# First operands of a merge split ahead of the last gate tile, in a longer-lived gate pool

## The chip, the cores and the metric

The kernel runs on one core of one Trainium2 chip. The metric is the device time of one execution in microseconds (us). Five engines work in parallel, each through its own list in order: PE (TensorE, matrix products), DVE (VectorE), ACT (ScalarE), POOL (GpSimd) and SP (SyncE, which here issues nearly all DMA transfers). They synchronise by semaphores.

## The reference

One inference step of a hybrid decoder layer (one layer here) for 1024 prompt tokens and 32 sampled tokens (8 sequences of 4), width 1024, float32:

```python
h = rmsnorm(x, norm_mix_w)
p = h @ w_in          # split into q, k, v | conv input u | z, a, b | gates g_a, g_b
o_a = stick_breaking(q, k, v)           # 8 heads of 64, causal
o_b = gated_delta(conv(u), z, a, b)     # 4 heads of 128
y_a = o_a.reshape(bsz, t_len, SB_DIM) @ w_pa.astype(F32)
y_b = o_b @ w_pb.astype(F32)
mix = (jax.nn.sigmoid(g_a) * y_a + jax.nn.sigmoid(g_b) * y_b) @ w_o.astype(F32)
x = x + mix
hm = rmsnorm(x, norm_mlp_w)
x = x + jnp.square(jax.nn.relu(hm @ w_up.astype(F32))) @ w_down.astype(F32)
```

In stick-breaking attention the weight of key j for query i is sigmoid(z_ij) times the product of (1 - sigmoid(z_ik)) over the keys k between j and i: a product scan in place of a softmax.

## The kernel before, in words

All 1056 tokens stand in the columns of transposed activations; the features are in the 128 partitions. The columns are cut into four chunks `CX` of 256, 256, 256 and 288. Every dense product keeps float32 accuracy by three products on PE: both operands are split into a high part (a copy by ACT, rounded to the matmul's type) and a low part (a subtraction by DVE, `x - hi`), and hi*hi, lo*hi and hi*lo are added in PSUM. So each operand needs an ACT copy and a DVE subtraction before its first use. For the weights `load_w` does this (tiles `ws`, `wh`, `wl`).

The stages that matter here:

- The gate projection. Sixteen tiles (8 feature tiles j, for gate A with b = 0 and gate B with b = 1), each of four chunks with 24 matmuls (`pd_g`). The input is `xh`, `xl` in the pool `xp`. Each result goes through a sigmoid into a tile `gt` and by DMA to DRAM (`gA_d`, `gB_d`). Tiles `gt` are in the pool `fk`, under the tag "ft" with four buffers, as are the transposed residual blocks `xs`, which are loaded (`xr`), transposed by DVE and stored (`xT_d`).
- The attention, 64 blocks (head h, query block i). A block is: score products `sc`, ACT's sigmoid into `s`, a mask and `1 - s` on POOL (`am`), the product scan `pr` and a product with `s` on DVE, PE's transposes into `wt` (evacuated by ACT), and the products with the values, `po`, which ACT copies into a staging tile `oT` of the head. After the fourth copy of a head two DMA stores take `oT` to `o_d`. `pipeline` runs the blocks with fills between them: five gate tiles and the residual blocks up to block 34 (`SPLIT`), after that the second merge.
- The second merge, w_pb (tiles `pb`). Its operand is the delta-net branch, `o_d[4:8]`, loaded per chunk as `ofb0` to `ofb3` and split into `obh`, `obl`. Result times gate B goes into `tb`. It is called second after its place in the formula; in time it comes before the other.
- The first merge, w_pa (tiles `pa`), whose operands are `oa0` to `oa2` (loaded as `ofa0` to `ofa2`, split into `oah`, `oal`) and `oa3`, which the last attention heads write directly. Then `w_o`, the norm and the MLP.

Nothing in the code orders the engines' lists by hand. The tile framework plans them: it simulates the program with its own times and puts each engine's instructions in the order in which they come up, with some raised by `tc.high_priority()`. A tile that reuses the memory of another waits for the last reader of that one, a DMA store included. Pools are stacked, so where a pool is opened decides its address, and when it is closed what may follow there.

Of the kernel before, what the change touches and what calls it, by code (L numbers as in the profile page):

```python
# [8 lines left out]
F32 = mybir.dt.float32  # L9
F32R = mybir.dt.float32r  # L10
I32 = mybir.dt.int32
I64 = mybir.dt.int64
AF = mybir.ActivationFunctionType
ALU = mybir.AluOpType
# [4 lines left out]
P = 128  # L19
# [3 lines left out]
T = NP + NS  # L23
# [3 lines left out]
CX = [(0, 256), (256, 256), (512, 256), (768, 288)]  # L27
# [5 lines left out]
NC = NP // P  # L33
# [5 lines left out]
def hybrid_step(ctx, tc, x_prompt, x_sample, cache_k, cache_v, page_table, state_conv, state_ssm,  # L39
# [7 lines left out]
    def pool(name, bufs=1, stack=ctx, side=None, space=None):  # L47
        kw = {} if space is None else {"space": space}
        if side is not None:
            kw["side"] = side  # L50
        return stack.enter_context(tc.tile_pool(name=name, bufs=bufs, reuse_waits="tile", **kw))

    cst = pool("cst")
    wctx = ExitStack()
    wpool = pool("wpool", 2, stack=wctx)
    kctx = ExitStack()
    keep = pool("keep", stack=kctx)
    dr = ctx.enter_context(tc.tile_pool(name="dr", bufs=1, space=DRAM))
# [33 lines left out]
    for t in range(9):  # L92
        xn = sp.tile([P, D], F32, tag="xn", name=f"xn{t}", bufs=7)
        n = P if t < 8 else NS
# [9 lines left out]
            w0s.append(st)  # L104
    ident = cst.tile([P, P], F32, name="ident")
    make_identity(nc, ident)
    ones = cst.tile([P, P], F32, name="ones")
    V.memset(ones, 1.0)
    powc = cst.tile([P, 2], F32, name="powc")
# [75 lines left out]
    xctx = ExitStack()  # L185
    zctx = ExitStack()
    zp = pool("zp", stack=zctx)
    xp = pool("xp", stack=xctx)
    xhc, xlc = [None] * 4, [None] * 4
    for c in (3, 2, 1, 0):  # L190
        xhc[c] = xp.tile([P, KT, CX[c][1]], F32R, name=f"xh{c}")
        xlc[c] = xp.tile([P, KT, CX[c][1]], F32R, name=f"xl{c}")
    fk = pool("fk", stack=xctx)
    w0 = []
    for t in range(9):
        n = P if t < 8 else NS
# [169 lines left out]
        return (1536 + i * P, f"u{name}", evac), cv  # L366

    def z_job(h):
        z = zp.tile([P, T + 48], F32, tag="zz", name=f"z{h}")[:, 0:T]

        def evac(c, o, n, pt):
            S_.activation(z[:, o:o + n], pt[:, :n], AF.Copy)
            if c == 3:
                S_.activation(z, z, AF.Silu)
                G.tensor_copy(zs[:, h, :], z[:, NP:T])
                SY.dma_start(z_d[h], z[:, 0:NP])

        return 3072 + h * P, f"z{h}", evac
# [424 lines left out]
    NFT = 4  # L803
# [189 lines left out]
    def values_of(blk):  # L993
        hh, i = blk
        p, a = hh // 2, hh % 2
        vn = vns[p]
        if hh < 6:
            if i % 2 == 0:
                return
            m = i // 2  # L1000
            if m == 0:
                oTs[hh] = ak.tile([P, NC // 2, P], F32, tag="oT", name=f"oT{hh}")
            rs = slice(64 * a, 64 * a + 64)
            po = gtile(f"po{hh}_{m}")
            for b in range(2 * m + 2):
                for r in range(2):
                    if b > 2 * m + r:
                        continue
                    PE.matmul(po[64 * r:64 * r + 64, 0:P], lhsT=vn[:, b, rs], rhs=wts[hh, 2 * m + r][:, b * P:(b + 1) * P],  # L1009
                              start=(b == 0), stop=(b == 2 * m + r))  # L1010
            S_.activation(oTs[hh][:, m, :], po[:, 0:P], AF.Copy)
            if m == NC // 2 - 1:
                for r in range(2):
                    SY.dma_start(o_d[p, rs, 0:NP].rearrange("d (m r c) -> d r m c", r=2, c=P)[:, r],
                                 oTs[hh][64 * r:64 * r + 64])
            return
        if a == 0:
            return
        po = gtile(f"po6_{i}")
        for b in range(i + 1):  # L1020
            for x in range(2):
                rs = slice(64 * x, 64 * x + 64)
                PE.matmul(po[rs, 0:P], lhsT=vn[:, b, rs], rhs=wts[6 + x, i][:, b * P:(b + 1) * P], start=(b == 0), stop=(b == i))
        cs_ = slice(i * P, (i + 1) * P)
        S_.activation(oah3[:, cs_], po[:, 0:P], AF.Copy)
        V.tensor_tensor(oal3[:, cs_], po[:, 0:P], oah3[:, cs_].bitcast(F32), op=ALU.subtract)
# [30 lines left out]
    def pipeline(x0, x1, fill):  # L1057

        done = 0
        for x in range(x0, x1):  # L1060
            stage_a(x + LAG)
            upto = len(fill) * (x + 1 - x0) // (x1 - x0)
            stage_b(x, fill[done:upto])
            done = upto
# [14 lines left out]
    def residual_step(t):  # L1079
        n = P if t < 8 else NS  # L1080
        xn = ak.tile([P, D], F32, tag="xr", name=f"xr{t}", bufs=1)
        SY.dma_start(xn[:n], x_prompt[0, t * P:(t + 1) * P, :] if t < 8 else x_sample.rearrange("s t d -> (s t) d"))

        xs = fk.tile([P, D], F32, tag="ft", name=f"xs{t}", bufs=NFT)
        V.transpose(xs[:n], xn[:n])
        for a in range(n // 32):
            o = t * P + 32 * a
            SY.dma_start(xT_d[:, :, o:o + 32].rearrange("k (b i) j -> i (k b) j", i=32),
                         xs[32 * a:32 * a + 32].rearrange("i (b j) -> i b j", j=32))
# [16 lines left out]
    for x, (j, b) in enumerate(gjobs[11:]):  # L1106
        for c in range(len(CX)):
            fills.append(lambda j=j, b=b, c=c: gate_step(j, b, c))
            t = 4 * x + c
            if t % 2 == 1 and t >= 3:  # L1110
                fills.append(lambda t=(t - 3) // 2: residual_step(t))
    pipeline(0, SPLIT, fills)
    ofb0 = zp.tile([P, 4, 256], F32, tag="zz", name="ofb0")
    SY.dma_start(ofb0, o_d[4:8, :, 0:256].rearrange("k p c -> p k c"))
    xctx.close()
    tbctx = ExitStack()
    oa3 = pool("oa3", stack=tbctx)
# [17 lines left out]
    tbs = [tbp.tile([P, T], F32, name=f"tb{j}") for j in range(KT)]  # L1135
    obctx = ExitStack()
    obp = pool("obp", stack=obctx)
    obh, obl = [None] * 4, [None] * 4

    def ob_tiles(c):  # L1140
        obh[c] = obp.tile([P, 4, CX[c][1]], F32R, name=f"obh{c}")
        obl[c] = obp.tile([P, 4, CX[c][1]], F32R, name=f"obl{c}")

    for c in range(len(CX)):
        ob_tiles(c)
    for c, (o, n) in enumerate(CX):
        if c == 0:
            st = ofb0
        else:
            if c == 1:  # L1150
                st = z2p.tile([P, 4, 288], F32, tag="zz", name="ofb1")[:, :, 0:256]
            elif c == 2:
                st = obp.tile([P, 4, 256], F32, name="ofb2")
            else:
                st = z2p.tile([P, 4, 288], F32, tag="zz", name="ofb3")
            mark = SY.dma_start(st, o_d[4:8, :, o:o + n].rearrange("k p c -> p k c"))
        with tc.high_priority():
            S_.activation(obh[c], st, AF.Copy)
            V.tensor_tensor(obl[c], st, obh[c].bitcast(F32), op=ALU.subtract)
        if c == 2:  # L1160
            for j in range(2):
                SY.dma_start(tbs[j], gB_d[j])
# [39 lines left out]
    gap = pool("gap", 2, stack=gaps, side="right")  # L1202
    oA = [None] * 3 + [(oah3, oal3)]
    for k in range(3):
        oh = oap.tile([P, T], F32R, name=f"oah{k}")
        ol = oap.tile([P, T], F32R, name=f"oal{k}")
        if k == 2:
            st = oap.tile([P, T], F32, name="ofa2")
            SY.dma_start(st, o_d[k])
        else:  # L1210
            st = ofa[k]
        S_.activation(oh, st, AF.Copy)
        V.tensor_tensor(ol, st, oh.bitcast(F32), op=ALU.subtract)
        oA[k] = (oh, ol)
# [25 lines left out]
    gaps.close()  # L1240
    oactx.close()
    tbctx.close()
    zctx.close()

    kctx.close()
# [481 lines left out]
```

## Time and profile before

| | before |
|---|---|
| runs | 1691.89, 1692.62, 1697.1 us (median 1692.62) |
| profiled execution | 1702.95 us |
| its span (first to last instruction) | 1701.2 us |
| granted TensorE clock, mean | 0.994 |
| busy: PE, DVE, ACT, POOL | 97%, 69%, 46%, 14% |

The profiled execution is a run of its own, 10.3 us over the median of the others. A start time is given in us from the start of the span. A row of the timeline names start, duration, engine, source line, operation, output<-inputs and shape; rows of the same kind next to each other are joined ("x4"). In brackets stand the idle time of the engine ahead of it and what ended it. SPq is the queue of SP, where a DMA transfer is issued; it takes longer to land.

### The profile page before, as it was taken

Reading aid. Unit: us, or ns where it says so; the run is one execution under the profiler, and the core shown is the slowest. Engines: PE = TensorE matmul, PEld = TensorE weight load, DVE = VectorE, ACT = ScalarE, POOL = GpSimd, SP = SyncE. Lnnn points to the kernel's source line nnn. Section 1 sums busy time; section 2 is a strip of 40 time slices with the busy share of each in tenths; the row PEclk is TensorE's granted clock in tenths of the full one; section 3 lists DMA queues with packets and bytes.
Section 4 is the critical chain, followed back from the end, with each engine's and each line's share of the span. In section 5 each row is a group of like instructions: output and inputs, shape, how many; then the busy total and the mean of one; then the engine's idle time right before and its main releaser. Section 6 shows DMA issues by size and latency. Waiting matters only on the chain.

```text
span 1701.2 us, 34901 instructions
## 1 busy us (share of the span) xinstructions
PE 1656.6 (97%) x14046; PEld 1603.9 (94%) x14046; DVE 1174.4 (69%) x2363; ACT 778.3 (46%) x1556; POOL 229.7 (14%) x249
## 2 busy tenths in 40 slices
PE   7999999999999999999999999999999999999998
PEld 6999999999998789988999999999999999999998
DVE  6666676877334327889776488887777688688964
ACT  5453434343424225555533356554445563444455
POOL 2120111110004226665300000000000000000000
PEclk9999999999999999999999999999999999999999
DMA  5142233235537567996144645455443665442232
GB/s 182 38 119 81 69 95 106 86 112 147 153 99 216 156 176 168 217 239 190 26 146 131 177 134 146 148 149 172 152 150 115 233 224 208 158 159 97 96 113 78
DMA packets 260207, 240.88 MB, mean 142 GB/s; under 512 B 55907, under 2 KB 217796, under 8 KB 260045
## 3 DMA queue, kind: packets, MB, share of 16 engines
q1 hardware_dynamic: 255094, 227.90, 44.6%
q0 software_dynamic: 3200, 10.52, 2.1%
q8 instruction: 110, 1.80, 0.5%
q10 hardware_dynamic: 1750, 0.23, 0.1%
q14 instruction: 53, 0.43, 0.1%
HBM read 164.02 MB, written 74.58 MB: 140 GB/s over the span
## 4 chain that ended last, share of the span: by engine, by line
PE 86%; DVE 7%; DMA 4%; issue 2%; ACT 1%; SPq 0%; DVEq 0%; POOLq 0%; ACTq 0%
PE pu L142 6%; PE pu L141 6%; PE pu L140 6%; PE pw L142 5%; PE pw L140 5%; PE pw L141 5%; PE pd_g L140 4%; PE pd_g L142 4%; PE pd_g L141 4%; PE wt L114 2%; PE po L1009 1%; PE px L141 1%; PE px L140 1%; PE px L142 1%; PE pa L141 1%
## 5 line engine op out<-in xcount | busy, mean ns | idle before, releaser
L141 PE MATMUL pu<-Xl,uh 128*128 128x272 f32 (+1 forms) x812 | 230.4, 284 | 0.0
L142 PE MATMUL pu<-Xh,ul 128*128 128x272 f32 (+1 forms) x812 | 229.3, 284 | 0.5 <-DVE ul L1272 0.5
L140 PE MATMUL pu<-Xh,uh 128*128 128x272 f32 (+1 forms) x812 | 229.5, 283 | 0.0
L140 PE MATMUL pw<-hc,w 128*128 128x272 f32 (+1 forms) x784 | 219.4, 284 | 2.4 <-ACT w L1536 2.4
L141 PE MATMUL pw<-hc,w 128*128 128x272 f32 (+1 forms) x784 | 219.4, 284 | 0.0
L142 PE MATMUL pw<-hc,w 128*128 128x272 f32 (+1 forms) x784 | 212.6, 284 | 1.5 <-DVE w L1537 1.5
L142 PEld LDWEIGHTS pu<-Xh,ul 128*128 128x128 f32 x812 | 152.8, 189 | 0.7 <-DVE ul L1272 0.7
L140 PEld LDWEIGHTS pu<-Xh,uh 128*128 128x128 f32 x812 | 152.8, 188 | 0.1
L141 PEld LDWEIGHTS pu<-Xl,uh 128*128 128x128 f32 x812 | 152.7, 188 | 0.0
L140 PEld LDWEIGHTS pw<-hc,w 128*128 128x128 f32 x784 | 148.1, 189 | 2.8 <-ACT w L1536 2.6
L140 PE MATMUL pd_g<-xh,wh_g 128*128 128x256 f32 (+1 forms) x512 | 149.7, 292 | 1.1 <-issue 1.1
L142 PE MATMUL pd_g<-xh,wl_g 128*128 128x256 f32 (+1 forms) x512 | 148.9, 291 | 1.2 <-issue 1.2
L141 PE MATMUL pd_g<-xl,wh_g 128*128 128x256 f32 (+1 forms) x512 | 149.2, 291 | 0.0
L141 PEld LDWEIGHTS pw<-hc,w 128*128 128x128 f32 x784 | 147.2, 188 | 0.0
L142 PEld LDWEIGHTS pw<-hc,w 128*128 128x128 f32 x784 | 144.3, 189 | 1.9 <-DVE w L1537 1.9
L140 PEld LDWEIGHTS pd_g<-xh,wh_g 128*128 128x128 f32 x512 | 97.7, 191 | 4.8 <-issue 4.3
L971 DVE TENSOR_TENSOR_SCAN pr<-am 128x127 f32<-128x127 f32 (+7 forms) x64 | 89.8, 1404 | 15.5 <-POOL am L967 11.7
L141 PEld LDWEIGHTS pd_g<-xl,wh_g 128*128 128x128 f32 x512 | 97.7, 191 | 2.9 <-issue 2.6
L142 PEld LDWEIGHTS pd_g<-xh,wl_g 128*128 128x128 f32 x512 | 97.6, 191 | 2.9 <-issue 2.7
L1536 ACT ACTIVATE w<-a 128x512 fp32r<-128x512 f32 x84 | 46.7, 620 | 97.3 <-PE pw L142 87.3
L1509 ACT ACTIVATE hc<-hc 128x528 fp32r<-128x528 f32 x98 | 62.0, 643 | 28.9 <-DMA hc<-hc_d 27.2
L967 POOL TENSOR_SCALAR am<-s 128x128 f32<-128x128 f32 (+7 forms) x64 | 71.8, 1122 | 11.0 <-DVE pr L971 5.8
(588 smaller groups left out, 5058.1 us busy)
## 6 DMA issues: line engine op xcount, KB each, us to landing
hc<-hc_d SPq DMA_DIRECT2D x94, 264.0 KB
hc_d<-t SPq DMA_DIRECT2D x14, 952.0 KB
a<-in_w_down_dram SPq DMA_DIRECT2D x52, 256.0 KB
hc_d<-t SPq DMA_DIRECT2D x13, 896.0 KB
ws_c<-in_w_in_dram SPq DMA_DIRECT2D x16, 512.0 KB
ws_wo<-in_w_o_dram SPq DMA_DIRECT2D x32, 256.0 KB
ua<-in_w_up_dram SPq DMA_DIRECT2D x16, 512.0 KB
ub<-in_w_up_dram SPq DMA_DIRECT2D x16, 512.0 KB
```

Source lines behind the costliest of these rows:

```text
L114: return PE.transpose(out, in_, ident[:k, :k])
L140: PE.matmul(pt[:, :n], lhsT=wh[k], rhs=xh[k], start=(k == 0), stop=False)
L141: PE.matmul(pt[:, :n], lhsT=wh[k], rhs=xl[k], start=False, stop=False)
L142: PE.matmul(pt[:, :n], lhsT=wl[k], rhs=xh[k], start=False, stop=(k == nk - 1))
L967: G.tensor_scalar(am[:, :n], s[:, :n], -1.0, 1.0, op0=ALU.mult, op1=ALU.add)
L971: V.tensor_tensor_scan(pr[:, n - 1:0:-1], am_r, am_r, 1.0, op0=ALU.mult, op1=ALU.bypass)
L1009: PE.matmul(po[64 * r:64 * r + 64, 0:P], lhsT=vn[:, b, rs], rhs=wts[hh, 2 * m + r][:, b * P:(b + 1) * P], start=(b == 0), stop=(b == 2 * m ...
L1509: S_.activation(tl[:, 0], tl[:, 1].bitcast(F32), AF.Copy)
L1536: S_.activation(tl[:, 0], src, AF.Copy)
```

## The change

1. The pool `fk` is opened below the projection's input pool `xp`, with a context of its own, and stays open until the end of the first merge. So its four "ft" slots outlive `xp`.
2. A function `first_ob` loads `ofb0` and splits it into two "ft" tiles, `ob0False` (high) and `ob0True` (low). It is a fill four places ahead of the end of the list of fills, ahead of the third chunk of the last gate tile. Before, load and split stood after the pipeline's first part.
3. Other operands move into the "ft" slots: the staging tile `ofb2`, and the high and low parts of `oa0` and `oa1`. Their former pools shrink.
4. The staging tile `oT` gets `bufs=1`; its pool's default is 2.
5. Padding: `z` tiles shrink by 32 words, `wpad` in the first weight pool and `obpad` in `obp` are 32 words each and cleared by DVE. The addresses of the first pools move by 128 bytes.

```diff
@@ pools at the start
     wpool = pool("wpool", 2, stack=wctx)
+    wpad = wpool.tile([P, 32], F32, name="wpad", bufs=1)
...
     make_identity(nc, ident)
+    V.memset(wpad, 0.0)
...
     zp = pool("zp", stack=zctx)
+    fkctx = ExitStack()
+    fk = pool("fk", stack=fkctx)
     xp = pool("xp", stack=xctx)
...
-    fk = pool("fk", stack=xctx)
...
-        z = zp.tile([P, T + 48], F32, tag="zz", name=f"z{h}")[:, 0:T]
+        z = zp.tile([P, T + 16], F32, tag="zz", name=f"z{h}")[:, 0:T]
@@ values_of
-                oTs[hh] = ak.tile([P, NC // 2, P], F32, tag="oT", name=f"oT{hh}")
+                oTs[hh] = ak.tile([P, NC // 2, P], F32, tag="oT", name=f"oT{hh}", bufs=1)
@@ fills
+    obh, obl = [None] * 4, [None] * 4
+
+    def ob_split(c, st):
+        with tc.high_priority():
+            S_.activation(obh[c], st, AF.Copy)
+            V.tensor_tensor(obl[c], st, obh[c].bitcast(F32), op=ALU.subtract)
+
+    def first_ob():
+        st = zp.tile([P, 4, 256], F32, tag="zz", name="ofb0")
+        SY.dma_start(st, o_d[4:8, :, 0:256].rearrange("k p c -> p k c"))
+        for half_ in (obh, obl):
+            half_[0] = fk.tile([P, 4, 256], F32R, tag="ft", name=f"ob0{half_ is obl}", bufs=NFT)
+        ob_split(0, st)
+
+    fills.insert(len(fills) - 4, first_ob)
     pipeline(0, SPLIT, fills)
-    ofb0 = zp.tile([P, 4, 256], F32, tag="zz", name="ofb0")
-    SY.dma_start(ofb0, o_d[4:8, :, 0:256].rearrange("k p c -> p k c"))
     xctx.close()
@@ second merge
-    obh, obl = [None] * 4, [None] * 4
+    V.memset(obp.tile([P, 32], F32, name="obpad"), 0.0)
...
-    for c in range(len(CX)):
+    for c in range(1, len(CX)):
         ob_tiles(c)
...
-                st = obp.tile([P, 4, 256], F32, name="ofb2")
+            st = fk.tile([P, 4, 256], F32, tag="ft", name="ofb2", bufs=NFT)
...
@@ first merge
-        oh = oap.tile([P, T], F32R, name=f"oah{k}")
-        ol = oap.tile([P, T], F32R, name=f"oal{k}")
+        oh, ol = (fk.tile([P, T], F32R, tag="ft", name=f"oa{x}{k}", bufs=NFT) if k < 2
+                  else oap.tile([P, T], F32R, name=f"oa{x}{k}") for x in "hl")
...
     tbctx.close()
+    fkctx.close()
     zctx.close()
```

The number of instructions stays the same but for two DVE memsets. Their order changes in many places; three follow.

The first is ACT's list where the first copy into `oT` of head 1 stands (numbers in names are head and block; the last number counts tiles). Before:

```order
L983 ACTIVATE wt1_2_8234<-wt1_2_0_8235 128x384 [waits PE_49,Activation_49]
L1011 ACTIVATE oT1_8240<-po1_0_8241 128x128 [waits PE_49]
L1071 ACTIVATE gt0_6_8094<-pd_g0_6_2_8246 128x256 [waits PE_49]
L963 ACTIVATE s1_7_8272<-sc1_7_0_8273,sbb_4702 128x512 [waits DVE_49,PE_49,Pool_49]
L963 ACTIVATE s1_7_8272<-sc1_7_512_8277,sbb_4702 128x512 [waits PE_49]
```

After, where two DMA queues (`DMAHW5`, `DMAHW6`) are among the semaphores that the copy waits for:

```order
L986 ACTIVATE wt1_2_8236<-wt1_2_0_8237 128x384 [waits PE_49,Activation_49]
L1014 ACTIVATE oT1_8242<-po1_0_8243 128x128 [waits DMAHW5_49,DMAHW6_49,PE_49,Activation_49]
L966 ACTIVATE s1_7_8274<-sc1_7_0_8275,sbb_4704 128x512 [waits DVE_49,PE_49,Pool_49]
L966 ACTIVATE s1_7_8274<-sc1_7_512_8279,sbb_4704 128x512 [waits PE_49]
L986 ACTIVATE wt1_3_8289<-wt1_3_0_8290 128x512 [waits PE_49]
```

The copy `oT1` now waits for the two stores of head 0; the sigmoid `s1_7`, which frees the score product's bank, stays right behind it.

The second is the end of the gate. DVE's list before, with the low halves of chunks 0 and 1, `obl0` and `obl1`, among the scans of head 4's blocks 6 and 7:

```order
L971 SCALAR_TENSOR_TENSOR pr4_5_9334<-am4_5_9332 128x767
L972 TENSOR_TENSOR s4_5_9322<-s4_5_9322,pr4_5_9334 128x767
L971 SCALAR_TENSOR_TENSOR pr4_6_9413<-am4_6_9411 128x895
L1159 TENSOR_TENSOR obl0_9378<-ofb0_9347,obh0_9377 128x1024
L972 TENSOR_TENSOR s4_6_9401<-s4_6_9401,pr4_6_9413 128x895
L1159 TENSOR_TENSOR obl1_9380<-ofb1_9387,obh1_9379 128x1024
L971 SCALAR_TENSOR_TENSOR pr4_7_9440<-am4_7_9438 128x1023
L1177 TENSOR_TENSOR tb0_9366<-pb0_0_9456,tb0_9366 128x256
```

After, with chunk 0 (`ob0True`) behind block 5 of head 3, and chunks 2 and 1 ahead of block 4 of head 4:

```order
L975 TENSOR_TENSOR s3_5_8968<-s3_5_8968,pr3_5_8980 128x767
L1120 TENSOR_TENSOR ob0True_9168<-ofb0_9165,ob0False_9167 128x1024
...
L133 TENSOR_TENSOR wl_pb1_9802<-ws_pb1_9799,wh_pb1_9801 128x1024
L1120 TENSOR_TENSOR obl2_9387<-ofb2_9394,obh2_9386 128x1024
L1141 TENSOR_TENSOR oal3_9360<-ofs_9367,oah3_9359 128x32
L1120 TENSOR_TENSOR obl1_9385<-ofb1_9390,obh1_9384 128x1024
L1188 TENSOR_TENSOR tb0_9371<-pb0_0_9459,tb0_9371 128x256
L974 SCALAR_TENSOR_TENSOR pr4_4_9277<-am4_4_9275 128x639
L975 TENSOR_TENSOR s4_4_9265<-s4_4_9265,pr4_4_9277 128x639
```

So chunk 0's low half moves up past nine blocks, and `obl1` past three; `obl2` follows from further down. On ACT the same place reads, before:

```order
L1011 ACTIVATE oT3_9007<-po3_2_9186 128x128 [waits PE_49]
L963 ACTIVATE s4_4_9257<-sc4_4_512_9262,sbb_4702 128x128 [waits PE_49]
L983 ACTIVATE wt3_7_9218<-wt3_7_0_9219 128x512 [waits PE_49,Activation_49]
L983 ACTIVATE wt3_7_9218<-wt3_7_4_9225 128x512 [waits PE_49]
L130 ACTIVATE wh_pb1_9798<-ws_pb1_9796 128x1024 [waits DMAHW3_49,PE_49]
L1071 ACTIVATE gt1_7_9084<-pd_g1_7_3_9295 128x288 [waits PE_49]
```

and after:

```order
L966 ACTIVATE s4_4_9265<-sc4_4_0_9266,sbb_4704 128x512 [waits DVE_49,Pool_49]
L1014 ACTIVATE oT3_9009<-po3_2_9194 128x128 [waits PE_49]
L1119 ACTIVATE obh2_9386<-ofb2_9394 128x1024 [waits DMAHW1_49]
L1140 ACTIVATE oah3_9359<-ofs_9367 128x32 [waits DMAHW2_49]
L966 ACTIVATE s4_4_9265<-sc4_4_512_9270,sbb_4704 128x128 [waits PE_49]
L1119 ACTIVATE obh1_9384<-ofb1_9390 128x1024 [waits DMAHW3_49]
L986 ACTIVATE wt3_7_9226<-wt3_7_0_9227 128x512 [waits PE_49,Activation_49]
```

The copies `obh2` and `obh1`, each waiting for a DMA queue, come to stand ahead of the evacuation `wt3_7`. On SP the loads of `ofb2` and `ofb1` stand right behind the store of the last residual block, and the stores of `oT3` and `oT4` behind more loads (`tb`, `vn`, `ws_pb3`) than before.

The third is the start of the first merge on DVE. Before:

```order
L1177 TENSOR_TENSOR tb7_9373<-pb7_3_10684,tb7_9373 128x288
L1272 TENSOR_TENSOR wl_wo01_11429<-ws_wo010_11430,wh_wo01_11428 128x512
L131 TENSOR_TENSOR wl_pa1_10890<-ws_pa1_10887,wh_pa1_10889 128x1024
L1213 TENSOR_TENSOR oal0_10724<-ofa0_10703,oah0_10723 128x1056
L1213 TENSOR_TENSOR oal1_10728<-ofa1_10705,oah1_10727 128x1056
L1272 TENSOR_TENSOR wl_wo01_11429<-ws_wo011_11434,wh_wo01_11428 128x512
L1213 TENSOR_TENSOR oal2_10732<-ofa2_10733,oah2_10731 128x1056
```

After:

```order
L1188 TENSOR_TENSOR tb7_9378<-pb7_3_10687,tb7_9378 128x288
L133 TENSOR_TENSOR wl_pa1_10893<-ws_pa1_10890,wh_pa1_10892 128x1024
L1284 TENSOR_TENSOR wl_wo00_11365<-ws_wo000_11366,wh_wo00_11364 128x512
L1284 TENSOR_TENSOR wl_wo00_11365<-ws_wo001_11370,wh_wo00_11364 128x512
L1224 TENSOR_TENSOR oal2_10735<-ofa2_10736,oah2_10734 128x1056
```

Of the three low halves, `oal0` to `oal2`, one is left there. `oal0` now stands at head 4's block 5, `oal1` among the last `tb` products.

More of the change, by code (lines that the diff above doesn't have):

```diff
@@ L1142, in ob_tiles @@
         obl[c] = obp.tile([P, 4, CX[c][1]], F32R, name=f"obl{c}")
-    for c in range(len(CX)):
+    for c in range(1, len(CX)):
         ob_tiles(c)
-    for c, (o, n) in enumerate(CX):
-        if c == 0:
-            st = ofb0
-        else:
-            if c == 1:
-                st = z2p.tile([P, 4, 288], F32, tag="zz", name="ofb1")[:, :, 0:256]
-            elif c == 2:
-                st = obp.tile([P, 4, 256], F32, name="ofb2")
[L1154 to L1159, printed above, removed]
+    for c, (o, n) in list(enumerate(CX))[1:]:
+        if c == 1:
+            st = z2p.tile([P, 4, 288], F32, tag="zz", name="ofb1")[:, :, 0:256]
+        elif c == 2:
+            st = fk.tile([P, 4, 256], F32, tag="ft", name="ofb2", bufs=NFT)
+        else:
+            st = z2p.tile([P, 4, 288], F32, tag="zz", name="ofb3")
+        mark = SY.dma_start(st, o_d[4:8, :, o:o + n].rearrange("k p c -> p k c"))
+        ob_split(c, st)
         if c == 2:
```

## The prediction

> **What bounds the kernel now.** I read the page first, for the engine that bounds the whole.
>
> ```profile
> span 1701.2 us, 34901 instructions
> PE 1656.6 (97%) x14046; PEld 1603.9 (94%) x14046; DVE 1174.4 (69%) x2363; ACT 778.3 (46%) x1556; POOL 229.7 (14%) x249
> PE 86%; DVE 7%; DMA 4%; issue 2%; ACT 1%; SPq 0%; DVEq 0%; POOLq 0%; ACTq 0%
> ```
>
> The reader is to see that PE (TensorE) is busy for 97% and carries 86% of the chain that ended last. The change takes no matmul away, so it can pay only where PE stands still or runs at a lower clock, and can cost only by adding such places. So the second view is the windows, cut into the stages around the change (columns: stretch, its length, busy time of PE, PEld, DVE, ACT, POOL, then the granted clock, DMA share, GB/s).
>
> ```profile
> 690.00:745.00 55.00, 55.00 (x486) 50.85 (x485) 44.50 (x40) 31.67 (x70) 30.99 (x33) 1.00 0.91 212
> 745.00:757.50 12.50, 12.48 (x110) 10.53 (x108) 10.80 (x11) 9.18 (x19) 6.87 (x8) 1.00 0.79 229
> 757.50:765.00 7.50, 5.23 (x23) 4.33 (x23) 7.50 (x5) 3.03 (x8) 7.41 (x5) 0.77 1.09 311
> 765.00:800.00 35.00, 33.08 (x263) 28.13 (x262) 33.56 (x34) 18.05 (x35) 18.52 (x18) 1.00 0.73 205
> 800.00:850.00 50.00, 50.00 (x476) 45.87 (x475) 38.62 (x53) 25.20 (x54) 21.24 (x30) 1.00 0.13 38
> 860.00:870.00 10.00, 8.32 (x54) 7.68 (x53) 7.70 (x10) 5.24 (x6) 0.00 (x0) 0.87 0.75 248
> 870.00:880.00 10.00, 10.00 (x81) 9.98 (x81) 8.40 (x23) 4.08 (x9) 0.00 (x0) 0.96 0.41 128
> ```
>
> PE is full until 757.5, and from 800 to 850. It loses in two spots. Spot A is 757.5 to 800, the start of the second merge (the w_pb product, tiles `pb`): idle 7.50 - 5.23 = 2.27 us and 35.00 - 33.08 = 1.92 us, and the clock of 0.77 takes 0.23 x 7.50 = 1.7 us more. DVE is saturated there, 7.50 of 7.50 and 33.56 of 35. Spot B is the start of the first merge (tiles `pa`): idle 1.68 us, and clock 0.13 x 10 + 0.04 x 10 = 1.7 us. The waits of PE name what is late, first for 745 to 800, then for 855 to 880 (columns: us in total, times, longest):
>
> ```profile
> PE pb L141 <- DVE obl L1159: 2.8, 2, 2.1
> PE pb L140 <- DVE tb L1177: 1.1, 2, 0.9
> PE pb L140 <- ACT obh L1158: 0.2, 1, 0.2
> PE pa L140 <- ACT oah L1212: 0.8, 1, 0.8
> PE pa L141 <- DVE oal L1213: 0.7, 1, 0.7
> PE pa L140 <- DVE tb L1177: 0.2, 1, 0.2
> ```
>
> The timeline shows the largest of them, two rows of DVE and four of PE (start, us, operation, and in brackets the idle time before):
>
> ```profile
> 757.07 2.02 DVE L971 TENSOR_TENSOR_SCAN pr<-am 128x895 f32<-128x895 f32 x1
> 759.01 1.99 DVE L1159 TENSOR_TENSOR obl<-ofb,obh 128x1024 fp32r<-128x1024 f32 x1
> ...
> 761.05 0.39 PE L141 MATMUL pb<-obl,wh_pb 128*128 128x256 f32 x1 [2.10 <-DVE obl L1159]
> 763.01 0.41 PE L142 MATMUL pb<-obh,wl_pb 128*128 128x256 f32 x1
> ...
> 765.86 0.28 PE L140 MATMUL pb<-obh,wh_pb 128*128 128x256 f32 x1
> 765.98 0.28 PE L141 MATMUL pb<-obl,wh_pb 128*128 128x256 f32 x1
> ```
>
> The low half of chunk 0 stands on DVE behind a scan of 2.02 us, PE waits 2.10 us for it, and then runs nine steps in 1.96 us, 0.218 each, where 0.12 is the pace at full clock. So this one wait costs 2.1 us of idle time and 1.7 us of clock.
>
> **The change part by part.**
>
> *The early split of chunk 0.* Load, ACT copy and DVE subtraction (1.99 us in the row above) stand in the new order before the gate's end, where PE has its gate matmuls, and the `pb0_0` steps can run as soon as the gate is done. The 2.1 us, the 0.2 us of `obh` and the 1.7 us of clock go: 4.0. The rest of A, 1.9 us idle, is a full DVE's (0.7 for `obl`, 1.1 for `tb`). Its work before 800 changes little: 1.99 us moves ahead of the gate's end, 1.25 us of `oal0` (the size of `oal2`, row below) moves in from spot B. But DVE now has `obl2` and `obl1` ahead of block 4's scan of head 4 and so waits there for two loads. Bounds for what stays of 1.9 us: 0, and 1.9 or somewhat more; I take 1.9. Spot A gives 5.9 - 1.9 = 4.0.
>
> *The first merge.* `oa0` and `oa1` are now split early, in gate slots, `oa0` in A and `oa1` between 800 and 850, where DVE is busy 38.62 of 50 and PE full. What is left for the start of the merge on DVE are the last `tb` product, `wl_pa1`, both halves of `wl_wo`, and `oal2`:
>
> ```profile
> 862.99 0.29 PE L140 MATMUL pa<-oah,wh_pa 128*128 128x272 f32 x1
> 863.19 0.46 DVE L1177 TENSOR_TENSOR tb<-pb,tb 128x288 f32<-128x288 f32 x1 [1.17 <-PE pb L142]
> 863.56 0.68 DVE L1272 TENSOR_TENSOR wl_wo<-ws_wo,wh_wo 128x512 fp32r<-128x512 f32 x1
> 864.16 1.22 DVE L131 TENSOR_TENSOR wl_pa<-ws_pa,wh_pa 128x1024 fp32r<-128x1024 f32 x1
> 868.24 1.25 DVE L1213 TENSOR_TENSOR oal<-ofa,oah 128x1056 fp32r<-128x1056 f32 x1
> ```
>
> By starts that is 863.56 + 1.2 + 2 x 0.65 = 866.0, and `oal2` is done at 867.3. PE has three of the four operands and so 27 matmuls at 0.12, until 862.99 + 3.25 = 866.2. It waits 1.1 us, and about 0.2 for `tb` as before. The two `tb` waits of 1.1 us above left the clock at 1.00 in their window, so I charge none: B costs 1.3 instead of 3.4 and gives 2.1. Bounds: all 3.4, and nothing.
>
> *The single attention buffer.* The pool of gate tiles lives longer, and the attention output's staging tile `oT` gets one buffer instead of two. The first copy of head h into `oT` now waits on ACT until both stores of head h-1 have landed, and ACT runs its list in order: behind it stand the sigmoids that free the score banks. This is in no word of the description, and it is the main cost. For head 1, before:
>
> ```profile
> 668.06 0.28 ACT L1011 ACTIVATE oT<-po 128x128 f32<-128x128 f32 x1 [1.22 <-PE po L1009]
> 672.57 0.28 ACT L1011 ACTIVATE oT<-po 128x128 f32<-128x128 f32 x1
> 674.79 1.57 SPq L1088 DMA_DIRECT2D xT_d<-xs  x3
> 676.46 1.32 SPq L1014 DMA_DIRECT2D o_d<-oT  x2
> 676.00:680.00 4.00, 4.00 (x40) 3.84 (x40) 3.69 (x4) 3.29 (x7) 3.29 (x2) 1.00 1.07 184
> 677.69 0.22 PE L961 MATMUL sc<-kh,qs 128*128 128x128 f32 x1
> ```
>
> Head 0's last copy starts at 668.06 and head 1's first at 672.57, but the stores stand in SP's queue behind three transfers of the transposed residual and are issued from 676.46 to 677.78. From about 675.3, when the first of the three is issued, there are 3 x 128 + 2 x 128 = 640 KB to move at 184 GB/s, 3.6 us, so they land near 680, an estimate; no row shows the landing itself. ACT therefore stands from 672.6 to about 680. PE runs on without ACT until it needs a score bank for the next head's first score product (677.69 before). In the new order it has ahead of that 35 gate matmuls, 4 score products and 4 transposes: 21 x 0.13 + 14 x 0.12 + 4 x 0.23 + 0.6 = 5.9 us, until 678.4 (the paces by starts: 0.12 for 256 columns above, 0.13 and 0.23 for 288 and 512 in the rows from 748.32 below, 0.6 my estimate for the transposes). ACT frees the bank one us after the landing, at 681: the copy of 0.28, and an estimated 0.7 for the sigmoid. PE is then idle for 2.6 us, ACT's backlog adds some 0.7, and a wait of this size, as the one of 2.10 us in A, takes 1.7 us of clock: 5.0. Bounds: 0, if the landing is at 677.4 or earlier, and 7, if it is 2 us later.
>
> By the Trainium skill, page "TensorE: Matmul & The Clock Gate", section "HAM oscillation — how this bites in real kernels", it takes a gap of more than about 3.4 us of TensorE idleness to throw the clock back to half. Here the trace disagrees: after 2.10 us idle the pace was 0.218 us for 0.12. By the page's rule the stall would cost 3.3 instead of 5.0, and the sum below would be -1.8 and the time 1690.8; I go by the trace.
>
> *The later heads and the gate's end.* At heads 2 and 3 the same wait stands, but PE comes 5 us later by then and the stores, which hang on SP's queue and the residual loads, do not, so its 5.9 us of cover should do. At head 4 and 5 the stores stand behind loads of `tb` and `ws_pb`. At the gate's end ACT now waits for chunks 2 and 1 (`ofb2`, `ofb1`) ahead of the copies for the attention:
>
> ```profile
> 748.32 0.30 PE L142 MATMUL pd_g<-xh,wl_g 128*128 128x288 f32 x1
> 748.46 0.39 PE L961 MATMUL sc<-kh,qs 128*128 128x512 f32 x1
> 748.69 0.40 PE L962 MATMUL sc<-kl,qs 128*128 128x512 f32 x1
> 749.04 0.43 SPq L1156 DMA_DIRECT2D ofb<-o_d  x1
> 752.50:757.50 5.00, 4.98 (x42) 3.77 (x40) 3.88 (x4) 4.63 (x9) 4.72 (x6) 1.00 1.02 386
> ```
>
> In the new order PE needs `obh1` after the work that ran till 748.5, a score block (2 x 0.23 and a smaller piece, 0.6) and twelve `pb` steps (12 x 0.12 = 1.4): 750.5, or 755.5 with 5 us of delay from head 1. `ofb2` in a gate slot waits for the last residual store, so I put both issues near 748 to 749, as the 749.04 of before; two loads of 512 KB at 386 GB/s take 2.7 us, so the landing is at 752 to 754, and `obh1` about 1 us later. With the delay this costs 0 to 1, without it 3 to 5 and the clock. For all of these places together I take 1.0; bounds 0 and 6.
>
> *Nothing else.* The two memsets of 128 bytes per partition on DVE lie where PE is full or the kernel is starting. The moved addresses change no shape; gate steps and merge steps, whose operands lie in different pools, run at the same pace, near 0.12 for 256 columns and 0.13 for 288, so I cost it at 0; no row shows a cost of the address itself. The MLP after 880 keeps its order.
>
> Sum: -4.0 - 2.1 + 5.0 + 1.0 = -0.1 us. The profiled execution took 1702.95 us, 10.3 over the median of the runs, 1692.62; so small a difference is carried over as it is: 1702.85 profiled, 1692.5 as median.
>
> **The rivals.** *The new waits stay under cover (faster).* The stores land by 677.4, or PE's 5.9 us are more than I count. Then the sum is -4.0 - 2.1 = -6.1, or -9.3 if both spots empty entirely: 1683.3 to 1686.5. For it: the DMA queues move 386 GB/s in 752.5 to 757.5, twice the rate I use. Against it: the stores aren't even issued before 676.46, and the order of SP there is the same.
>
> *The single buffer stalls at several heads (slower).* One mechanism, the same wait at heads 2 and 3: if the stores are delayed with PE, since their copies are, each head costs 2.6 + 1.7 = 4.3. With three such stalls, 0.7 and the gains of 6.1 it ends at 13.6 - 6.1 = +7.5, so 1700.1. It decides from 11.2 us lost, two and a half stalls. For it: DMA share 0.91 from 690 to 745, so stores land late. Against it: ACT is busy only 31.67 of 55 there, so the wait has room, and a delayed PE meets a queue that went on.
>
> *The wait only changes its name (same).* If head 1 costs nothing, PE arrives early at the gate's end and waits there for `ofb1` in place of `obl`: 4 + 1.7 lost of 6.1 gained: -0.4, 1692.2. Then the change doesn't do at spot A what it says.
>
> **How the numbers follow.** About 0.3%, 5.1 us, is what a measurement of this kernel can tell from no change: 1687.5 and 1697.7 are the borders. My forecast has 0.36, the changed name 0.15, both within the borders: 0.51. Covered waits 0.27, faster. Several stalls 0.22, slower. The range goes from 1685.0, over half of the covered case, to 1699.5, near three stalls; some 1 in 10 is left on each side. Taking the likeliest alone it is 1689 to 1696.
>
> **What would show it.** Right: spot A's row `PE pb <- DVE obl` of 2.8 us gone or under 1; spot B's idle near 1.3 us and its clock near 1.00; a PE wait of 2 to 4 us near 675 to 683, for ACT's `s` or the score bank, with a slow pace after it, and ACT idle some 7 us before the `oT` copy, ended by a DMA. Wrong: PE full from 670 to 690 (the first rival), such waits near 705 and 733 too (the second), or a new PE wait at 750 to 756 for `obh` (the third). A pace of the gate steps other than 0.12 and 0.13 would mean that the moved addresses matter after all.

## The result and the profile after

The changed kernel takes 1701.05 us in the median of 16 runs (1696.97 to 1712.98), the kernel before 1693.83 in the median of 16 runs alongside. The ratio is 1.0043, with a 95% interval of 1.0027 to 1.0058: 7.3 us slower (4.6 to 9.8). The forecast was 1692.5, no measurable change, with a range to 1699.5; the time lies outside. The profiled execution took 1710.86 us, near the upper end of its runs, with a span of 1709.2.

The page after, the same rows as before:

```profile
span 1709.2 us, 34919 instructions
PE 1660.0 (97%) x14046; PEld 1608.6 (94%) x14046; DVE 1172.4 (69%) x2365; ACT 777.5 (45%) x1556; POOL 220.3 (13%) x249
PE 75%; issue 12%; DVE 5%; DMA 5%; ACT 1%; SPq 1%; POOL 0%; DVEq 0%; POOLq 0%; ACTq 0%
```

PE is busy 3.4 us longer in a span 8.0 us longer, so 4.6 us, more than half of the loss, is idle time. (The 12% under "issue" is mainly one piece of 180 us in the MLP, from 1164.55, where the page doesn't follow the chain any further; PE is busy all through it, so it is no loss.) The windows after (columns as before: stretch, length, busy of PE, PEld, DVE, ACT, POOL, clock, DMA share, GB/s) show where it is lost:

```profile
690.00:705.00 15.00, 12.22 (x105) 11.04 (x105) 11.19 (x9) 4.54 (x10) 5.25 (x5) 1.00 0.68 164
705.00:745.00 40.00, 39.01 (x319) 36.40 (x320) 29.20 (x26) 22.43 (x51) 18.72 (x23) 0.91 0.88 203
745.00:757.50 12.50, 8.57 (x73) 7.53 (x71) 8.03 (x12) 5.03 (x11) 2.72 (x4) 0.95 0.77 171
757.50:765.00 7.50, 5.57 (x43) 4.75 (x43) 5.78 (x7) 4.77 (x9) 2.60 (x4) 0.63 1.03 387
765.00:800.00 35.00, 34.56 (x294) 30.74 (x293) 31.51 (x33) 20.86 (x42) 21.16 (x21) 1.00 0.71 205
800.00:850.00 50.00, 44.91 (x401) 41.55 (x400) 40.79 (x45) 23.10 (x48) 25.07 (x28) 0.97 0.16 38
870.00:880.00 10.00, 9.14 (x70) 8.61 (x70) 6.73 (x13) 3.78 (x6) 0.00 (x0) 1.00 0.79 256
```

The stretch from 765 to 800, DVE's saturated one, is nearly full now (0.44 us idle in place of 1.92), and the first merge loses 0.86. But three places, 690 to 706, 745 to 765 and 800 to 850, have gaps that were not there, and the clock is lower behind them, most of all from 705 to 745 (0.91, up to 0.09 x 40 = 3.6 us). The waits of PE from 640 to 900 name them:

```profile
PE sc L964 <- DMA kh<-kh_d: 4.8, 1, 4.8
PE sc L964 <- ACT s L966: 4.4, 2, 3.9
PE pd_g L142 <- ACT gt L1074: 3.8, 1, 3.8
PE pb L142 <- ACT obh L1119: 1.9, 1, 1.9
PE pa L143 <- DVE oal L1224: 0.9, 1, 0.9
PE pb L142 <- DVE tb L1188: 0.7, 2, 0.4
```

They add up to 16.5 us, where the rows of before add up to 5.8. That is 10.7 us more, and from the first score product to the last step of the first merge, in both profiles, it is 10.5 more (303.3 and 313.8); PE is busy for about 297.6 us of that stretch in both. The stretch starts 4.2 us earlier after the change, so the span shows less than the 10.5. These are the rows of the tiles `sc` and `pa` (durations, first and last start), of before and then of after:

```profile
L961 PE MATMUL sc<-kh,qs x96: 221/388/775, 609.6 to 843.9; 128*128 128x512 f32 x48, 128*128 128x128 f32 x16, 128*128 128x256 f32 x16, 128*128 128x384 f32 x16
L142 PE MATMUL pa<-oah,wl_pa x128: 277/284/428, 851.7 to 912.9; 128*128 128x256 f32 x64, 128*128 128x272 f32 x64
```

```profile
L964 PE MATMUL sc<-kh,qs x96: 221/390/767, 605.4 to 852.8; 128*128 128x512 f32 x48, 128*128 128x128 f32 x16, 128*128 128x256 f32 x16, 128*128 128x384 f32 x16
L144 PE MATMUL pa<-oah,wl_pa x128: 277/284/291, 860.7 to 919.2; 128*128 128x256 f32 x64, 128*128 128x272 f32 x64
```

The four timelines of the changed kernel behind these waits: PE's gaps, then ACT, then SP, with two rows of SP from before at the end.

```profile
675.21 0.33 PE L964 MATMUL sc<-kh,qs 128*128 128x128 f32 x1 [0.52 <-ACT s L966]
705.99 0.58 PE L142 MATMUL pd_g<-xh,wh_g 128*128 128x256 f32 x1 [3.77 <-ACT gt L1074]
756.82 0.58 PE L964 MATMUL sc<-kh,qs 128*128 128x256 f32 x1 [3.93 <-ACT s L966]
759.55 0.58 PE L142 MATMUL pb<-obh,wh_pb 128*128 128x256 f32 x1 [1.93 <-ACT obh L1119]
807.48 1.19 PE L964 MATMUL sc<-kh,qs 128*128 128x512 f32 x2 [4.82 <-DMA kh<-kh_d]
```

```profile
674.30 0.28 ACT L1014 ACTIVATE oT<-po 128x128 f32<-128x128 f32 x1 [5.35 <-DMA o_d<-oT]
705.36 0.28 ACT L1014 ACTIVATE oT<-po 128x128 f32<-128x128 f32 x1 [6.42 <-DMA o_d<-oT]
755.34 1.06 ACT L1119 ACTIVATE obh<-ofb 128x1024 fp32r<-128x1024 f32 x1 [4.99 <-DMA ofb<-o_d]
758.44 1.06 ACT L1119 ACTIVATE obh<-ofb 128x1024 fp32r<-128x1024 f32 x1 [1.67 <-DMA ofb<-o_d]
```

```profile
670.99 1.32 SPq L1017 DMA_DIRECT2D o_d<-oT  x2
699.40 1.29 SPq L1017 DMA_DIRECT2D o_d<-oT  x2
745.33 0.32 SPq L1091 DMA_DIRECT2D xT_d<-xs  x1
751.37 0.39 SPq L1169 DMA_DIRECT2D ofb<-o_d  x1
752.36 0.42 SPq L1169 DMA_DIRECT2D ofb<-o_d  x1
790.29 0.39 SPq L128 DMA_DIRECT2D ws_pb<-in_w_pb_dram  x1
794.35 0.49 SPq L884 DMA_DIRECT2D kh<-kh_d  x1
```

```profile
782.58 0.48 SPq L881 DMA_DIRECT2D kh<-kh_d  x1
796.40 0.39 SPq L126 DMA_DIRECT2D ws_pb<-in_w_pb_dram  x1
```

The reader is to see three new waits. **The single buffer:** ACT stands 5.35 and 6.42 us ahead of the first copy into `oT` of heads 1 and 2, until a store has landed, and PE runs dry for 0.52 and 3.77 us. **The gate's end:** ACT stands 4.99 us for `ofb2` and 1.67 us for `ofb1`; behind these copies are the evacuations and sigmoids that PE needs, and it idles 3.93 and 1.93 us, with a clock of 0.63 after it. `ofb2` needs the gate slot of the last residual block and is issued only at 751.37, 6 us after that block's store, and `ofb1` behind it. **Head 7's loads:** SP issues them at 794.35, after `ws_pb3` at 790.29, which had to wait for its buffer, and four transfers behind that one; before the change they came first, at 782.58, and `ws_pb3` last, at 796.40. PE idles 4.82 us.

### The profile page after: what moved, and what is told of

It reads as the page before. It is cut to its first block, busy times and chain, and to the rows that moved or that the text cites. A ratio compares the mean times of both kernels' runs of the same rounds, so it can differ in the third digit from the quotient of the medians.

```text
span 1709.2 us, 34919 instructions
## 1 busy us (share of the span) xinstructions
PE 1660.0 (97%) x14046; PEld 1608.6 (94%) x14046; DVE 1172.4 (69%) x2365; ACT 777.5 (45%) x1556; POOL 220.3 (13%) x249
## 4 chain that ended last, share of the span: by engine, by line
PE 75%; issue 12%; DVE 5%; DMA 5%; ACT 1%; SPq 1%; POOL 0%; DVEq 0%; POOLq 0%; ACTq 0%
PE pw L144 5%; PE pw L143 5%; PE pw L142 5%; PE pd_g L142 4%; PE pd_g L143 4%; PE pd_g L144 3%; PE pu L144 3%; PE pu L142 2%; PE pu L143 2%; PE wt L116 1%; PE px L143 1%; PE po L1012 1%; PE px L142 1%; PE px L144 1%; DMA kh<-kh_d 1%
## 5 line engine op out<-in xcount | busy, mean ns | idle before, releaser
L142 PE MATMUL pw<-hc,w 128*128 128x256 f32 (+1 forms) x784 | 219.8, 284 | 2.5 <-ACT w L1548 2.4
L143 PE MATMUL pw<-hc,w 128*128 128x256 f32 (+1 forms) x784 | 220.1, 284 | 0.0
L144 PE MATMUL pw<-hc,w 128*128 128x272 f32 (+1 forms) x784 | 214.0, 284 | 0.6 <-DVE w L1549 0.6
L143 PE MATMUL px<-ml,wh_wo 128*128 128x256 f32 (+1 forms) x256 | 72.6, 284 | 0.0
```

Source lines behind the costliest of these rows:

```text
L142: PE.matmul(pt[:, :n], lhsT=wh[k], rhs=xh[k], start=(k == 0), stop=False)
L143: PE.matmul(pt[:, :n], lhsT=wh[k], rhs=xl[k], start=False, stop=False)
L144: PE.matmul(pt[:, :n], lhsT=wl[k], rhs=xh[k], start=False, stop=(k == nk - 1))
```

## The experiments

Every ratio is to the kernel before on the same chip, with five rounds each. The runs were made on several chips (e1 to e4 on one, e5 to e7 and e11 on another, e8 to e10 on a third), so ratios are compared here and not times. The last five columns are idle times of PE in us by place, summed from each profile's waits between 640 and 900.

| | ratio (95%) | heads 1, 2 | gate's end | head 7 | first merge | later DVE `tb`, `obl` |
|---|---|---|---|---|---|---|
| before | 1 | 0 | 2.3 | 0 | 1.7 | 1.8 |
| changed kernel | 1.0043 (1.0027 to 1.0058) | 4.3 | 5.9 | 4.8 | 0.9 | 0.7 |
| e2: before, one `oT` buffer | 1.0030 (1.0014 to 1.0045) | 4.7 | 2.3 | 0 | 1.7 | 2.0 |
| e1: changed, two buffers | 1.0035 (1.0020 to 1.0050) | 0 | 6.4 | 4.2 | 2.4 | 0.7 |
| e8: e1 with padding | 1.0045 (1.0029 to 1.0061) | 0 | 6.9 | 3.1 | 2.1 | 1.4 |
| e3: changed, head 7 first | 1.0014 (1.0002 to 1.0025) | 4.2 | 4.7 | 2.6 | 0.9 | 1.4 |
| e4: e1 and e3 | 1.0012 (1.0001 to 1.0023) | 0 | 8.1 | 2.1 | 2.3 | 0.9 |
| e9: e4 with padding | 1.0024 (1.0010 to 1.0039) | 0 | 6.3 | 2.3 | 2.2 | 1.4 |
| e6: e4, late split | 1.0010 (0.9995 to 1.0025) | 0 | 4.1 | 2.2 | 2.4 | 1.6 |
| e5: e4, `ofb1` first | 0.9996 (0.9980 to 1.0012) | 0 | 2.4 | 2.1 | 2.3 | 1.0 |
| e7: e5, one buffer | 1.0030 (1.0012 to 1.0047) | 3.2 | 0.7 | 1.7 | 2.0 | 1.1 |
| e10: e5 with padding | 0.9999 (0.9983 to 1.0015) | 0 | 1.4 | 2.0 | 2.6 | 2.1 |
| e11: e10, `ofa2` first | 0.9987 (0.9974 to 0.9999) | 0 | 2.5 | 1.9 | 0 | 1.0 |

**e1, two buffers in the changed kernel.** One operand tile moves into the idle slot of the residual loads to make room; the order of the engines stays, but for one ACT copy.

```diff
-  oTs[hh] = ak.tile([P, NC // 2, P], F32, tag="oT", name=f"oT{hh}", bufs=1)
+  oTs[hh] = ak.tile([P, NC // 2, P], F32, tag="oT", name=f"oT{hh}")
-  obh[c] = obp.tile([P, 4, CX[c][1]], F32R, name=f"obh{c}")
+  obh[c] = (ak.tile([P, 4, 256], F32R, tag="xr", name="obh2", bufs=1) if c == 2
+            else obp.tile([P, 4, CX[c][1]], F32R, name=f"obh{c}"))
```

> The changed kernel with two oT buffers again (one operand tile, obh2, lies in the slot of the residual loads to make room); the order of all engines is that of the changed kernel but for one copy of head 4. Theory 1, the single buffer is the main loss: no wait of ACT for the stores of oT, the PE gap of 3.8 us at 706 and its slow clock go, 7 us less than the changed kernel, about 1694 us, ratio to before near 1.000. Theory 2, the gate's end and the queue of SP set the time: PE only arrives earlier and waits longer at the gate's end and for head 7's loads, so 0 to 2 us less, about 1699 to 1701, ratio near 1.004.

Measured: 1.0035. The waits at heads 1 and 2 are gone, and the time hardly moves. Theory 1 fails for the changed kernel as it stands.

**e2, one buffer in the kernel before.** The edit is the first line of e1, the other way round; the order stays but for three ACT copies.

> The kernel before with one oT buffer and nothing else; the order is that of before but for three copies of heads 4 and 5. Theory 1: slower by about 7 us, ratio 1.004, with ACT idle ahead of the first copy of heads 1 to 3 until a store lands, and a PE gap of some 4 us with a slow clock after it. Theory 2: the waits lie within what PE has to do meanwhile, ratio 1.000 to 1.001.

Measured: 1.0030, some 5 us. Its profile has the mechanism alone (ACT, SP, PE, and the window of it):

```profile
681.01 0.28 ACT L1011 ACTIVATE oT<-po 128x128 f32<-128x128 f32 x1 [8.18 <-DMA o_d<-oT]
677.68 1.32 SPq L1014 DMA_DIRECT2D o_d<-oT  x2
682.19 0.33 PE L961 MATMUL sc<-kh,qs 128*128 128x128 f32 x1 [4.13 <-ACT s L963]
```

```profile
665.00:690.00 25.00, 20.87 (x168) 19.04 (x167) 19.39 (x18) 10.21 (x24) 11.99 (x13) 0.93 0.77 164
```

The stores are issued from 677.68 to 679.00, ACT is released at 681.01, and PE has idled 4.13 us; 0.07 x 25 = 1.75 us of clock follow. Heads 2 and 3 cost 0.58 and nothing. So the buffer has its price, but whether the kernel pays it depends on what else it waits for.

**e3, head 7's loads first.** The edit, shortened, moves three rows of SP's queue, `ws_pb3` and two `tb` loads behind it, and two score products of PE change places; the other lists stay as they are in the stretch looked at.

```diff
+  hmark[0] = SY.dma_start(...)        # the last load of a head, in fetch_head
-  wbs[jp] = load_w(wpbv[:, :, jp * 256:(jp + 1) * 256], f"pb{jp}")
+  with (tc.issue_after(hmark[0].ins) if jp == 3 else ExitStack()):
+      wbs[jp] = load_w(wpbv[:, :, jp * 256:(jp + 1) * 256], f"pb{jp}")
```

> The changed kernel with one row of SP's queue moved: the weight load ws_pb3, which waits for its buffer, stands behind the loads of head 7 in place of ahead of them. If the queue is a loss of its own (theory 2): the PE gap of 4.8 us at 807 goes, and with its clock 5 to 6 us, about 1695 us, ratio 1.001. If the loads of head 7 are late because all that is before is late (theory 1): 0 to 2 us, ratio 1.003 to 1.004.

Measured: 1.0014, 4.9 us less than the changed kernel, and the wait for head 7 falls from 4.8 to 2.6. Its profile shows 3.7 of these 4.9 us at head 7: 2.2 us of idle time, and 0.03 x 50 = 1.5 us of clock from 800 to 850, where it is 1.00 now. Of the two edits made to the changed kernel alone, e1 and e3, this one gives back the most.

**e4, both.** Beside e3 only one copy of ACT changes its place.

> The changed kernel with two oT buffers and with head 7's loads ahead of ws_pb3. If the two losses add: about 12 us less than the changed kernel, 1688 us, ratio to before 0.997. If they replace each other: about the better of the two single ones, 1694 us, ratio 1.000. What the gate's end costs beside them is then seen in its profile: with 4 to 6 us of PE idle at 745 to 765 it is a third loss.

Measured: 1.0012. They replace each other: without the wait at heads 1 and 2 PE comes to the gate's end earlier and waits there 8.1 us in place of 4.7.

```profile
750.28 0.58 PE L966 MATMUL sc<-kh,qs 128*128 128x256 f32 x1 [5.88 <-ACT s L968]
753.28 0.58 PE L142 MATMUL pb<-obh,wh_pb 128*128 128x256 f32 x1 [2.20 <-ACT obh L1121]
```

**e5, `ofb1`'s load ahead of `ofb2`'s,** added to e4.

```diff
-  mark = SY.dma_start(st, o_d[4:8, :, o:o + n].rearrange("k p c -> p k c"))
+  with (tc.issue_after(mark.ins) if c == 2 else ExitStack()):
+      mark = SY.dma_start(st, o_d[4:8, :, o:o + n].rearrange("k p c -> p k c"))
```

> Two oT buffers, head 7's loads ahead of ws_pb3, and now also the load of ofb2, which waits for a gate slot until the last residual store has landed, stands behind the load of ofb1 in SP's queue. Theory: the 8.1 us that PE is idle at the gate's end in the kernel with both edits, and the clock of 0.73 there, come from ofb1 being queued behind that wait; then most of it goes, 5 to 8 us less, ratio to before 0.996 to 0.998. Rival: the loads are late because the DMA engines still move head 5's loads at 200 GB/s then; the load is issued earlier but lands as late, 0 to 2 us less, ratio 1.000 to 1.001.

Measured: 0.9996; the gate's end falls from 8.1 to 2.4 us idle. The intervals of e4 and e5 overlap, and less is won than expected: 2.7 us by the two ratios, with e9 and e10 4.2. The second pair runs the same lists as the first at other addresses, so both measure the same edit. PE's list stays the same until behind these waits (742 us); from there on the planner orders it anew, so the time need not be that of the one load alone.

**e6, the early split undone,** added to e4: `first_ob()` is called behind `pipeline(0, SPLIT, fills)` and is no fill any more.

> The kernel with two oT buffers and head 7's loads ahead of ws_pb3 (ratio 1.0012), with first_ob called behind the first part of the pipeline in place of four fills ahead of its end; the operands stay in the gate slots. The planner puts the low half of chunk 0 three blocks later and runs no pb step ahead of the last blocks of head 3. If the early split pays by itself: slower than that kernel by 2 to 4 us, ratio about 1.003. If what matters at the gate's end is when chunks 1 and 2 land: the same within 1 us, ratio 1.001.

Measured: 1.0010, as e4. But the edit undoes the early split only in part. DVE makes the low half of chunk 0 at 737.80 in place of 726.38, still ahead of the last gate steps, and seven of the twelve steps of chunk 0 still run ahead of the wait at the gate's end, where ACT stands 6.64 us for the load of a later chunk. The planner also orders PE's list anew from 651 us on. So a split some 11 us later does not cost time here; the idle time at the gate's end is 4.1 us against 8.1, and what the early split, the aim of the change, is worth by itself no run shows.

**e7, one buffer again,** added to e5, with `obh2` back in its pool.

> As the kernel with all three edits, but with one oT buffer. If the wait at the gate's end had covered the cost of the single buffer (which cost 5 us in the kernel before and 0 to 1.4 us in the changed one): 4 to 6 us slower than with two buffers, ratio about 1.000. If the single buffer costs little in this order of work by itself: 0 to 1.5 us slower, ratio 0.997 to 0.998.

Measured: 1.0030, against 0.9996 with two: 5.8 us by the ratios, as expected. The profiles show less of it. Heads 1 and 2 idle 3.2 us, the gate's end 1.7 us less than in e5, and from the first score product to the last step of the first merge it is only 1.5 us more. The first score product itself starts 4.7 us later, behind a stretch (400 to 605) with a clock of 0.97 where e5 has 1.00, and ahead of any use of `oT`; from some 760 us on the order differs too. So it is likely that the buffer has a price in this order as well, but its size is not shown.

**e8, e9, e10: padding.** I took the late first merge of e1 to come from `ofa2`, whose memory there lay over an operand that is read until the last `pb` step. `obpad` grows from 32 to 96 words, added to e1, e4 and e5.

> The changed kernel with two oT buffers again, as in the first experiment, but with 256 bytes of padding more in obp. In that first one the moved operand tile had put the load of ofa2 over memory that is read until the last pb step, so the first merge waited 1.8 us for oah2, with its clock, a cost of the experiment and not of the buffer. Theory: without that the second buffer is worth what it cost in the kernel before, 4 to 5 us: ratio 1.0015 to 1.002. Rival: the gate's end takes back what the buffer gives: ratio 1.0035 as in the first experiment.

> Two oT buffers and head 7's loads ahead of ws_pb3, with the padding. Theory, the losses add: 3 us less than without the padding, ratio 0.9990 to 0.9997. Rival, they replace each other: ratio 1.001 as without it.

> Two oT buffers, head 7's loads ahead of ws_pb3, ofb1's load ahead of ofb2's, with the padding. Theory: all three losses and the late ofa2 gone, only the gains of the change are left (spots A and B of the kernel before, 4 to 9 us): ratio 0.9970 to 0.9985. Rival: the delayed PE had given DVE and the loads time, and PE waits for DVE between 765 and 800 instead: ratio 0.9995 as without the padding.

Measured: 1.0045, 1.0024, 0.9999, none better than without the padding. My theory of e1's side effect fell: the first merge still idles 2.1 to 2.6 us. Two rows of SP, of e8 and of the changed kernel, show a second place of the same kind:

```profile
860.07 0.93 SPq L1293 DMA_DIRECT2D ws_wo<-in_w_o_dram  x2
861.10 0.44 SPq L1221 DMA_DIRECT2D ofa<-o_d  x1
```

```profile
853.50 1.01 SPq L1292 DMA_DIRECT2D ws_wo<-in_w_o_dram  x2
```

The last `pb` step starts at 862.3 and at 872.5, so `ws_wo` is issued 2.2 us ahead of it in e8 and 19.0 us in the changed kernel. `ofa2` stands behind it in the queue. That `ws_wo` lies over memory which is freed later, since the attention pool is larger with two `oT` buffers, is my reading; no run moves this memory alone. By it the second buffer loses some of its gain here.

**e11, `ofa2` ahead of `ws_wo`,** added to e10 (edit shortened).

```diff
+  with (tc.issue_after(omark.ins) if name == "wo00" else ExitStack()):   # omark: ofa2's load
       SY.dma_start(st, src[:, qs_, :])
```

> The kernel with two oT buffers, head 7's loads ahead of ws_pb3, ofb1's load ahead of ofb2's and the padding (ratio 0.9999), and now ofa2's load ahead of the two loads of ws_wo, whose buffer is free only after the last value products. If the 2.1 us for oah2 and 0.5 us for oal2 at the start of the first merge come from ofa2 being queued behind ws_wo: idle there under 1 us, 2 to 3 us less with its clock, ratio 0.998 to 0.9985, faster than before. If the landing of ofa2 is bound by its own 528 KB: the same idle, ratio 0.9995 to 1.000.

Measured: 0.9987 (0.9974 to 0.9999), 1690.26 us beside 1691.51 for the kernel before. The first merge has no idle time left:

```profile
850.00:880.00 30.00, 30.00 (x243) 29.67 (x244) 24.60 (x58) 12.21 (x26) 0.13 (x1) 1.00 0.62 197
```

It is the only version whose interval lies below 1, and only just; that of e10 overlaps with it. ACT's and DVE's lists change around the first merge too, and a few steps of the MLP.

## Why the prediction was wrong, point by point

**The step that failed** is "the later heads and the gate's end", taken as 1.0 us with bounds of 0 and 6. It was mis-sized, and a part of it was missing. In its place the profile has 3.8 us of idle time at head 2, 5.9 at the gate's end and 4.8 at head 7, 14.5 together; the 5.0 that I put on head 1 came to 0.5 idle.

- Head 2: I let the 5.9 us of cover do for it. They did not; the numbers stand under the single buffer below.
- Gate's end: I put the issues of `ofb2` and `ofb1` near 748 to 749 and the wait at 0 to 1 us, given the delay from head 1. They came at 751.37 and 752.36. The last residual store was issued at 745.33, behind six loads of head 5 at some 200 GB/s, and the slot was free only 6 us later. The wait was 5.9 us, and up to 0.37 x 7.5 = 2.8 us of clock (PE stood still for 1.93 of these 7.5 us). e4 and e5 show the cause: with `ofb1` ahead of `ofb2` the idle time falls from 8.1 to 2.4 us. The bounds of 3 to 5 without delay were too low as well: 6.4 and 8.1 in e1 and e4.
- Head 7's loads: no term had them. I had named `ws_pb` only as a load that the stores of `oT` stand behind, and did not follow who else did. PE waited 4.82 us for them; in e3, with the loads first, the kernel takes 4.9 us less, 3.7 of them at head 7 by the profile. This is the part that a walk along SP's queue, row by row behind every waiting transfer, would have given.

**The early split.** The rows that I said would go did go: `obl` no longer holds PE at chunk 0, and `tb` costs 0.7 us in place of 1.1. Of 1.9 us left I kept all; 0.7 remained. But the gain of 4.0 was not one: at the same place PE now waits 5.9 us for chunks 1 and 2 where it waited 2.3 us for chunk 0. Even with that wait down to 2.4 and 1.4 us (e5, e10) the time is only that of the kernel before.

**The first merge.** Expected 1.3 us idle and no clock lost: 0.86 and a clock of 1.00. Right, though by e8 and e11 it hangs on where `ws_wo` and `ofa2` lie.

**The single buffer.** Expected 5.0 us at head 1: 2.6 idle, 0.7 backlog, 1.7 clock. The mechanism is as described: ACT stands for a store, and PE for ACT. In the kernel before (e2) it is 4.13 idle and 1.75 clock, by time 0.3%. The working has a slip: 675.3 and 3.6 give a landing at 678.9, not 680. In e2 the copy began 2.0 us after the last store's issue, and from 677.78 that gives 679.8, so the 680 came out right without its sum. In the changed kernel the gap moved to head 2 (0.52 and 3.77). The stores of head 0 were issued 5.5 us sooner (670.99 and not 676.46) in a stretch that began 4.2 us sooner, and at head 2 the copy began 4.7 us after the last store's issue (700.69 to 705.36), not 2.0; e3 has gaps at both heads, 1.95 and 2.29. I had written that later heads should do with their cover; at head 2 they did not. With the clock, up to 3.6 us, both heads cost up to 7.9 us in this profile, over my bound of 7, though e1 gets back only 0.0008, 1.4 us. That the change's own order does not pay it in full (e1, e8) I had only as the rival "the wait only changes its name", with the single buffer costing nothing. It was the other way round: the buffer's wait came first and hid part of the gate's end (4.7 us with one buffer in e3, 8.1 with two in e4; 5.9 in the changed kernel, 6.4 in e1, where the first merge waits 1.5 us longer too).

**The chances.** 0.22 on slower went to three stalls of the same buffer; what came was three different waits.

**The moved addresses.** Costed at 0 as to pace, and the paces stayed (0.12 and 0.13 us for gate steps of 256 and 288 columns). As to waits, no run tests the addresses of the change itself. In e8, with another layout, `ws_wo` is issued 17 us later against the last `pb` step than in the changed kernel, so a layout can cost.

What stays open: e4 and e9, e1 and e8, and e5 and e10 differ only by padding (and were run on different chips) and lie 0.0003 to 0.0012 apart, within their intervals, so that single terms are known to about 2 us. The profile of before also idles on "issue", for nothing that the trace shows, ahead of the first score product, and that of after doesn't (609.6 against 605.4); nothing in the change explains it and no run here tested it. From 400 to 605 the clock is 0.99 before and 0.97 after, which is open in the same way.

## What to carry to other kernels

When a change moves one transfer up an in-order DMA queue, list everything behind it and when each is needed: here one weight load ahead of six head loads went with 4.8 us of idle time, more than the 4.0 us that the early operand was to give. A buffer taken from a ring hangs on the landing of the ring's slowest user; the price shows only where no other wait covers it, so test it in the old order and in the new. And the gain of an early operand can be taken back at the wait for the next one: here 2.3 us went and 5.9 came.

## What the runs showed of the hardware

- The time from a store's issue to the start of its waiter is not constant. In e2 the last store of `oT` was issued by 679.00, and the copy of head 1 began at 681.01, 2.0 us later; in the changed kernel it was 2.0 us at head 1 (672.31 to 674.30) and 4.7 us at head 2. The Trainium skill, page "DMA: Bandwidth & Descriptors", section "Anatomy of one DMA — SWDGE (gpsimd) path", gives about 2.0 us of fixed cost per transfer on the path of GpSimd, most of it the receipt from the target memory, and the time of the bytes on top. These stores are issued by SP and their 2.0 us hold the bytes too, so no run here tests that figure.
- The clock after a gap is not a matter of the gap's length alone: 1.95 us idle at head 1 in e3 left it at 1.00 (window below), 2.10 us in the kernel before took 1.7 us, 4.13 us in e2 took 1.75, and 3.77 us in the changed kernel up to 3.6. The Trainium skill, page "TensorE: Matmul & The Clock Gate", section "HAM oscillation — how this bites in real kernels", gives about 3.4 us of idle as the limit. The 2.10 us of before disagree with a limit on one gap.

```profile
665.00:690.00 25.00, 23.05 (x196) 21.31 (x195) 19.81 (x17) 12.71 (x28) 13.03 (x13) 1.00 0.87 200
```
